# The gate matrices of four tokens, written one token behind the other

## The chip, the core and the metric
The kernel runs on one core of a Trainium2 chip. The core has a matrix engine (TensorE, PE in the profile; its weight loads are listed apart as PEld), a vector engine (VectorE, DVE), a scalar engine (ScalarE, ACT), GpSimd (POOL) and a sync engine (SyncE, SP) that issues most of the DMAs. Each works through its own list of instructions in order and waits on semaphores for the others. The metric is the device time of one execution in microseconds; a run's time is compared by its median.

## The reference
The program is one layer of a hybrid encoder block on 512 tokens of width 1024: an attention part with two branches, and behind it a product-key retrieval (PEER). The change touches the retrieval alone:

```
v1, i1 = lax.top_k(s1, 16); v2, i2 = lax.top_k(s2, 16)      # per token and head, 128 keys each
top, ci = lax.top_k(v1[..., :, None] + v2[..., None, :], 16) # best 16 of the pairs
eidx = e1 * 128 + e2; gate = softmax(top)                    # 8 heads x 16 experts of 16384
act = gelu(einsum('td,thkd->thk', x, expert_u[eidx]))
y = einsum('thk,thkd->td', gate * act, expert_v[eidx])
```

For every token 128 experts (8 heads of 16) are chosen out of 16384, and their rows of `expert_u` and `expert_v` are used with the weights gate times gelu.

## The kernel before
The 512 tokens form four groups of 128. Group 0 is done by gathers: for each of its 128 slots an indirect DMA on GpSimd's queue fetches one row per token (512 KB in all), VectorE takes the dot product with the token (`dot`, L1065) or adds the weighted row to a sum (`add`, L1077). The other three groups (384 tokens) are done densely: all 16384 experts are gone through in 128 blocks of 128. A block's `uT` rows are multiplied with the tokens (24 matmuls `pj`, L86 to L88, three fp32r products of high and low halves), gelu gives `am`, this is multiplied with the block's gates, and the product with `expert_v` is summed up in PSUM (`y`, L1231).

For the dense part the gates of a token are needed as a matrix of 128 x 128, first key by second key. The gate stage makes them, in the loop `for t0 in range(0, 128, T)` (from L1127), 32 steps of T = 4 tokens for each of three groups, 96 steps in all. The 128 slots of a token lie on the partitions. In a step VectorE writes
- two tiles `oh` (L1135): one-hot rows, 1 where the slot's first (second) key is e, an fp16 tile [128, 128, T] with the four tokens innermost;
- two tiles `og` (L1140): the first one-hot times the slot's gate, whose high and low fp16 halves are `gp[0]` and `gp[1]`.

TensorE then makes eight matmuls (L1147), two for each token, which sum over the slots; the weights are `oh[1][:, :, q + j]`, the moving columns `pcs[i][:, :, q + j]`, both with a step of four elements (8 bytes). ScalarE copies the four matrices of the step out of PSUM into the tile `stage` (L1149), with the token as the innermost index. After eight steps SyncE writes `stage` to HBM as `gd` (L1157), and the expert_v stage reads it back in pieces, `gch` (L1175).

What runs beside it: `oh` and `og` have three buffers each (OB = 3). The first 64 of the dense blocks' `uT` half are done ahead, from L1152 (`run_ahead`), most of them within the gate stage: SyncE loads `raw`, ScalarE rounds it to `whi` (L91), VectorE or GpSimd computes the rest `wlo` (L92), TensorE makes the 24 `pj`, ScalarE the gelu (L879), and the result goes to HBM as `gls`. In the last third of the stage `eidx` of group 0 is computed (L1125) and its first 16 gathers and dots are put out.

The order of instructions on each engine is not the order of the code. A scheduler sets it when the program is built, by costs of its own for every instruction; only GpSimd's order in the expert_v stage is fixed by hand. So the scheduler may answer the change of one instruction with another order of all of them.

Of the kernel before, what the change touches and what calls it, by code (L numbers as in the profile page):

```python
# [18 lines left out]
HF = mybir.dt.float16  # L19
# [3 lines left out]
OP = mybir.AluOpType  # L23
# [872 lines left out]
def peer(K, A, out):  # L896
    nc, cst, gen, Pool = K.nc, K.cst, K.gen, K.Pool
# [4 lines left out]
    RT, OB, SB, J0, GB = 8, 3, 2, 16, 4  # L902
# [12 lines left out]
    def ptr():  # L915
        return pe_.tile([128, 512], F32, name="pt", bufs=2)

    def pg():
        return pe_.tile([128, 512], F32, name="pg", bufs=2)
# [41 lines left out]
    def run_ahead():  # L961
        if K.ahead < NS:
            K.run_ahead(pmat(), pa.tile([128, ND], F32, name="am", bufs=4), nc.vector)
# [58 lines left out]
    def slots(p, a):  # L1022
        rb = ranks(p, a).rearrange("p h f k -> p (h f) k")

        eq = p.tile([128, 16, 16, 16], BF, name="eq", bufs=1)
        for r in range(16):
            nc.vector.scalar_tensor_tensor(eq[:, r], rb, float(r), ib[:, a, :, r, None].to_broadcast([128, 16, 16]),
                                           op0=OP.is_equal, op1=OP.mult)
        ev = eq.rearrange("p r s k -> p r (s k)")
        n = 8  # L1030
        while n > 1:
            nc.vector.tensor_tensor(ev[:, 0:n], ev[:, 0:n], ev[:, n:2 * n], op=OP.add)
            n //= 2
        ef = p.tile([128, 2, 128], F32, name="ef", bufs=2)
        nc.vector.tensor_tensor(ef.rearrange("p f (h k) -> p h f k", k=16), eq[:, 0].rearrange("p (h f) k -> p h f k", f=2),
                                eq[:, 1].rearrange("p (h f) k -> p h f k", f=2), op=OP.add)
        e = [ef[:, f, :] for f in range(2)]
        g = p.tile([128, 8, 16], F32, name="gate", bufs=2)
        nc.vector.tensor_tensor(g, top[:, a], top[:, a, :, 0:1].to_broadcast([128, 8, 16]), op=OP.subtract)
        nc.scalar.activation(g, g, AF.Exp)  # L1040
        z = small(8)
        nc.vector.tensor_reduce(out=z, in_=g, op=OP.add, axis=AX)
        rz = small(8)
        nc.vector.reciprocal(rz, z)
        nc.vector.tensor_tensor(g, g, rz[:, :, None].to_broadcast([128, 8, 16]), op=OP.mult)
        return e[0], e[1], g.rearrange("p h k -> p (h k)")
# [41 lines left out]
    def run_jobs(done):  # L1088
        while jobs and njobs - len(jobs) < done:
            jobs.pop(0)()  # L1090


    gt = K.wk = Pool("gates")
    T = 4
# [4 lines left out]
    def gathered_heads(hs):  # L1099
        for h in hs:  # L1100
            s0 = gt.tile([128, 4, 128], F32, name="sc0", bufs=2)
            nc.sync.dma_start(s0, A['sc0'][:, 2 * h:2 * h + 4, :])
            pair_top(gt, 0, h, lambda hh, half: s0[:, 2 * hh + half, :], 1)

    for b, a in enumerate(DT):
        if b:
            gathered_heads(range(4 * b - 4, 4 * b, 2))
        tr = []
        for n, t in enumerate(slots(gt, a)):
            p = ptr()  # L1110
            nc.tensor.transpose(p[:, :128], t, ident)
            s = gt.tile([128, 128], HF if n < 2 else F32, name=f"sT{n}", bufs=2)
            nc.scalar.activation(s, p[:, :128], AF.Copy, scale=1.0 if n < 2 else GS)
            tr.append(s)
        gT = tr[2]
        gp = []
        for i in range(2):
            q = gt.tile([128, 128], HF, name=f"gp{i}", bufs=2)
            nc.vector.tensor_copy(q, gT)
            if i == 0:  # L1120
                nc.vector.tensor_tensor(gT, gT, q, op=OP.subtract)
            gp.append(q)
        if b == 2:
            e1, e2, g = slots(gt, 0)
            nc.vector.scalar_tensor_tensor(eidx, e1, 128.0, e2, op0=OP.mult, op1=OP.add)  # L1125
            nc.vector.tensor_copy(gate0, g)
        for t0 in range(0, 128, T):  # L1127
            ts = slice(t0, t0 + T)
            tb = t0 % 32
            if tb == 0:  # L1130
                st = gt.tile([128, 128, 32], F32, name="stage", bufs=SB)
            oh = []
            for i in range(2):
                o = gt.tile([128, 128, T], HF, name=f"oh{i}", bufs=OB)
                nc.vector.tensor_tensor(o, tr[i][:, None, ts].to_broadcast([128, 128, T]), iota, op=OP.is_equal)  # L1135
                oh.append(o)
            pcs = []
            for i in range(2):
                o = gt.tile([128, 128, T], HF, name=f"og{i}", bufs=OB)
                nc.vector.tensor_tensor(  # L1140
                    o, oh[0], gp[i][:, None, ts].to_broadcast([128, 128, T]), op=OP.mult)
                pcs.append(o)
            for q in range(0, T, 4):
                p = pg()
                for j in range(4):
                    for i in range(2):
                        nc.tensor.matmul(p[:, j * 128:j * 128 + 128], oh[1][:, :, q + j], pcs[i][:, :, q + j],  # L1147
                                         start=i == 0, stop=i == 1)
                nc.scalar.activation(st[:, :, tb + q:tb + q + 4].rearrange("p e t -> p t e"),  # L1149
                                     p.rearrange("p (t e) -> p t e", t=4), AF.Copy, scale=1 / GS)  # L1150
            if t0 % 16 == RT:
                run_ahead()  # L1152
            if b == 2:
                run_jobs(J0 * (t0 + T) // 128)
            if tb == 28:
                for c in range(4):
                    nc.sync.dma_start(gd[c][4 * b + t0 // 32].rearrange("c p e t -> p c (e t)"),  # L1157
                                      st[:, 32 * c:32 * c + 32, :].rearrange("p (c e) t -> p c (e t)", e=8))
# [90 lines left out]
def block(tc, A, out):  # L1249
    with ExitStack() as ctx:  # L1250
        dram = ctx.enter_context(tc.tile_pool(name="dram", bufs=1, space=bass.MemoryType.DRAM))
        A['x1d'] = dram.tile([128, 4, 1024], F32, name="x1d")
        A['gd'] = [dram.tile([12, 4, 128, 8, 32], F32, name=f"gd{c}") for c in range(4)]
        A['gls'] = dram.tile([128, 128, 384], F32, name="gls")
        A['sc0'] = dram.tile([128, 16, 128], F32, name="sc0d")
        K = Ctx()
        setup(tc, ctx, K)
        front(K, A)
        peer(K, A, out)
# [29 lines left out]
```

## Time and profile before

| | |
|---|---|
| median of 3 runs | 2042.31 us (2037.0 to 2042.57) |
| profiled execution | 2043.98 us, its span 2042.2 us |
| busy in the span | TensorE 1918.3 us, VectorE 1585.0, ScalarE 844.9, GpSimd 821.9 |
| gate stage, from the first `oh` to the end of the last `og` | 874.9 to 1158.2 us |
| first `y` matmul | 1193.87 us |

Times in the rows are counted from the start of the span. A busy TensorE is not TensorE at its peak: matmuls are pipelined, so a matmul's own duration is longer than the step from one start to the next. A row that merges several instructions in succession gives the time from the first start to the last end.

### The profile page before, as it was taken

How to read it: one execution, taken by the hardware profiler on the slowest of the kernel's cores; microseconds unless marked ns; L12 is line 12 of the kernel's file. 1: busy time of each engine (PE TensorE's matmuls, PEld its weight loads, DVE VectorE, ACT ScalarE, POOL GpSimd, SP SyncE). 2: the span in 40 equal slices, each digit the busy share in tenths (PEclk: the TensorE clock that was granted, in tenths of full speed). 3: DMA queues.
4: the chain of work that ended last, by engine and by line, in shares of the span. 5: the costliest groups of instructions: out<-in, count | busy, mean ns of one | idle time of the engine just before them, and what ended most of it. 6: DMA issues, size and time to landing. Idle time of an engine off the chain costs nothing.

```text
span 2042.2 us, 28294 instructions
## 1 busy us (share of the span) xinstructions
PE 1918.3 (94%) x9858; PEld 1659.9 (81%) x9858; DVE 1585.0 (78%) x3212; ACT 844.9 (41%) x1330; POOL 821.9 (40%) x598
## 2 busy tenths in 40 slices
PE   6999999989899899999999998989898999999998
PEld 5987777777777788999999986968787878888886
DVE  8488585887766658998888778677877888878787
ACT  3444445646533333455666532333332333333232
POOL 2554332352244531000000545455555565746474
PEclk9999999999999899999999999999999999999999
DMA  7334142122246322646656998797979898989886
GB/s 261 90 115 123 52 145 57 37 84 87 63 150 213 140 88 88 190 151 214 225 194 209 336 340 310 272 338 257 357 280 323 288 331 299 338 291 327 320 318 256
DMA packets 199952, 436.80 MB, mean 214 GB/s; under 512 B 16465, under 2 KB 97666, under 8 KB 199682
## 3 DMA queue, kind: packets, MB, share of 16 engines
q1 hardware_dynamic: 162128, 298.65, 43.4%
q0 software_dynamic: 36864, 134.23, 18.0%
q10 hardware_dynamic: 818, 2.12, 0.3%
q8 instruction: 77, 1.26, 0.2%
q14 instruction: 65, 0.53, 0.1%
HBM read 391.95 MB, written 42.99 MB: 213 GB/s over the span
## 4 chain that ended last, share of the span: by engine, by line
PE 34%; DMA 19%; DVE 10%; issue 10%; POOL 5%; ACT 1%; SPq 0%; DVEq 0%; POOLq 0%; ACTq 0%
PE pj L86 6%; PE y L1231 6%; PE pj L87 6%; PE pj L88 6%; DMA gat<-expert_v,eidx 5%; PE pg L1147 5%; DMA raw<-uT 3%; DMA gat<-expert_u,eidx 3%; DMA am<-gls 3%; POOL gat L1059 3%; DVE wlo L92 2%; DMA raw<-expert_v 2%; POOL wlo L92 2%; PE pq L86 1%; PE pq L88 1%
## 5 line engine op out<-in xcount | busy, mean ns | idle before, releaser
L91 ACT ACTIVATE whi<-raw 128x1024 fp32r<-128x1024 f32 (+3 forms) x431 | 383.6, 894 | 610.4 <-DMA raw<-expert_v 242.6
L92 POOL TENSOR_TENSOR wlo<-raw,whi 128x1024 fp32r<-128x1024 f32 (+2 forms) x156 | 316.4, 2032 | 406.4 <-ACT whi L91 375.9
L92 DVE TENSOR_TENSOR wlo<-raw,whi 128x1024 fp32r<-128x1024 f32 (+3 forms) x275 | 333.7, 1217 | 136.5 <-ACT whi L91 136.1
L1059 POOL DMA_INDIRECT gat<-expert_u,eidx x128 | 162.6, 1270 | 464.6 <-DVE eidx L1125 343.5
L86 PE MATMUL pj<-h2h,whi 128*128 128x384 f32 x1008 | 344.4, 342 | 1.0 <-ACT am L879 1.0
L88 PE MATMUL pj<-h2h,wlo 128*128 128x384 f32 x1008 | 343.3, 341 | 0.0
L87 PE MATMUL pj<-h2l,whi 128*128 128x384 f32 x1008 | 343.3, 341 | 0.0
L1231 PE MATMUL y<-whi,al 128*128 128x512 f32 x768 | 239.3, 403 | 32.0 <-DVE al L92 32.0
L1231 PE MATMUL y<-wlo,ah 128*128 128x512 f32 x768 | 246.1, 401 | 9.2 <-POOL wlo L92 7.9
L1231 PE MATMUL y<-whi,ah 128*128 128x512 f32 x768 | 248.0, 400 | 5.5 <-ACT ah L91 5.4
L1059 POOL DMA_INDIRECT gat<-expert_v,eidx x128 | 172.8, 1350 | 132.8 <-DVE acc L1077 73.6
L1231 PEld LDWEIGHTS y<-whi,al 128*128 128x128 f32 x768 | 144.2, 190 | 76.7 <-DVE al L92 43.1
L1065 DVE SCALAR_TENSOR_TENSOR gscr<-gat,h2tok 128x1024 bf16<-128x1024 f32 x128 | 178.7, 1396 | 32.5 <-DMA gat<-expert_u,eidx 31.9
L86 PE MATMUL pj<-whi,hh 128*128 128x512 f32 (+2 forms) x512 | 193.0, 390 | 11.0 <-DVE gA L651 4.4
L1077 DVE SCALAR_TENSOR_TENSOR acc<-gat,wts,acc 128x1024 f32<-128x1024 f32 x127 | 173.9, 1369 | 31.6 <-DMA gat<-expert_v,eidx 31.1
L87 PE MATMUL pj<-wlo,hh 128*128 128x512 f32 (+2 forms) x512 | 196.0, 383 | 2.4 <-DVE wlo L92 2.3
L86 PEld LDWEIGHTS pj<-h2h,whi 128*128 128x128 f32 x1008 | 190.9, 189 | 4.2 <-ACT am L879 1.3
L87 PEld LDWEIGHTS pj<-h2l,whi 128*128 128x128 f32 x1008 | 190.7, 189 | 2.5
L88 PE MATMUL pj<-whi,hl 128*128 128x512 f32 (+2 forms) x512 | 192.0, 382 | 0.0
L88 PEld LDWEIGHTS pj<-h2h,wlo 128*128 128x128 f32 x1008 | 190.6, 189 | 0.4
L1231 PEld LDWEIGHTS y<-wlo,ah 128*128 128x128 f32 x768 | 146.6, 191 | 45.6 <-POOL wlo L92 8.3
L1231 PEld LDWEIGHTS y<-whi,ah 128*128 128x128 f32 x768 | 145.2, 191 | 36.8 <-ACT ah L91 7.3
(313 smaller groups left out, 3207.8 us busy)
## 6 DMA issues: line engine op xcount, KB each, us to landing
raw<-uT SPq DMA_DIRECT2D x128, 512.0 KB, 4.4
raw<-expert_v SPq DMA_DIRECT2D x128, 512.0 KB, 6.2
gd<-stage SPq DMA_DIRECT2D x48, 512.0 KB, 4.4
gch<-gd SPq DMA_DIRECT2D x16, 1536.0 KB, 11.2
raw<-w_in SPq DMA_DIRECT2D x88, 256.0 KB, 2.8
raw<-w_ada SPq DMA_DIRECT2D x64, 256.0 KB, 2.8
am<-gls SPq DMA_DIRECT2D x64, 192.0 KB, 6.2
gls<-am SPq DMA_DIRECT2D x62, 192.0 KB, 2.0
```

The source lines that it names most:

```text
L86: nc.tensor.matmul(ps, lh, rh, start=start, stop=False)
L87: nc.tensor.matmul(ps, lh, rl, start=False, stop=False)
L88: nc.tensor.matmul(ps, ll, rh, start=False, stop=stop)
L91: nc.scalar.activation(hi, raw, AF.Copy)
L92: (eng or nc.vector).tensor_tensor(lo, raw, hi.bitcast(F32), op=OP.subtract)
L1059: nc.gpsimd.indirect_dma_start(out=t, out_offset=None, in_=src, in_offset=bass.IndirectOffsetOnAxis(ap=eidx[:, s:s + 1], axis=0))
L1065: nc.vector.scalar_tensor_tensor(scr, t, 1.0, h2tok, op0=OP.mult, op1=OP.mult, accum_out=act[:, s:s + 1])
L1077: nc.vector.scalar_tensor_tensor(acc, t, wts[:, s:s + 1], acc, op0=OP.mult, op1=OP.add)
L1147: nc.tensor.matmul(p[:, j * 128:j * 128 + 128], oh[1][:, :, q + j], pcs[i][:, :, q + j], start=i == 0, stop=i == 1)
L1231: nc.tensor.matmul(ys[b][n], l[:, bs], r[:, n * 512:n * 512 + 512], start=n_ == 0 and i == 0, stop=n_ == 127 and i == 2)
```

## The change
The two tiles `og` are laid out as [128, T, 128], one token's 128 columns behind the other's. The multiply that writes them reads `oh[0]` through a view with its last two dimensions exchanged, and the gate with the token as the outer dimension, repeated over the 128 columns. The matmul's moving operand is `pcs[i][:, q + j, :]`. The one-hot tiles, the weights of the matmul and everything behind it stay as they are.

```diff
-                o = gt.tile([128, 128, T], HF, name=f"og{i}", bufs=OB)
+                o = gt.tile([128, T, 128], HF, name=f"og{i}", bufs=OB)
                 nc.vector.tensor_tensor(
-                    o, oh[0], gp[i][:, None, ts].to_broadcast([128, 128, T]), op=OP.mult)
+                    o, oh[0].rearrange("p e t -> p t e"), gp[i][:, ts, None].to_broadcast([128, T, 128]), op=OP.mult)
                 pcs.append(o)
             for q in range(0, T, 4):
                 p = pg()
                 for j in range(4):
                     for i in range(2):
-                        nc.tensor.matmul(p[:, j * 128:j * 128 + 128], oh[1][:, :, q + j], pcs[i][:, :, q + j],
+                        nc.tensor.matmul(p[:, j * 128:j * 128 + 128], oh[1][:, :, q + j], pcs[i][:, q + j, :],
                                          start=i == 0, stop=i == 1)
```

The scheduler also puts the instructions in another order, from the start of the gate stage on. On VectorE the end of the gate stage reads so before (`og_10923` to `og_10977` are the last two steps' tiles, `gscr,act` the dots of group 0; `eidx` stands 48 rows ahead of the last row here):

```order
L1140 TENSOR_TENSOR og_10923<-oh_10919,gp_10023 128x512
L1140 TENSOR_TENSOR og_10925<-oh_10919,gp_10026 128x512
L1065 SCALAR_TENSOR_TENSOR gscr,act<-gat,h2tok 128x1024
L1135 TENSOR_TENSOR oh_10973<-sT_10017,iota 128x512
L1140 TENSOR_TENSOR og_10975<-oh_10971,gp_10023 128x512
L1140 TENSOR_TENSOR og_10977<-oh_10971,gp_10026 128x512
L1065 SCALAR_TENSOR_TENSOR gscr,act<-gat,h2tok 128x1024
L92 TENSOR_TENSOR wlo<-raw,whi 128x1024
```

and now:

```order
L1140 TENSOR_TENSOR og_10923<-oh_10919,gp_10023 128x512
L1140 TENSOR_TENSOR og_10925<-oh_10919,gp_10026 128x512
L1140 TENSOR_TENSOR og_10975<-oh_10971,gp_10023 128x512
L1140 TENSOR_TENSOR og_10977<-oh_10971,gp_10026 128x512
L1032 TENSOR_TENSOR eq<-eq 128x512
L1035 TENSOR_TENSOR ef<-eq 128x8x2x16
L1125 SCALAR_TENSOR_TENSOR eidx<-ef 128x128
L1065 SCALAR_TENSOR_TENSOR gscr,act<-gat,h2tok 128x1024 x5
L1212 TENSOR_TENSOR am<-am,gch 128x384 x4
```

The five dots that stood between the last `og`, and `eidx` on which all gathers depend, have moved behind the last `og`.

On TensorE the last matmuls of the gate stage (the pair of tile `oh_10973`) are followed before by

```order
L1147 LDWEIGHTS oh_10973
L1147 MATMUL pg<-og_10977,oh_10973 128x128
L87 MATMUL pj<-h2l_6198,whi 128x384
L88 MATMUL pj<-h2h,wlo 128x384
L86 MATMUL pj<-h2h,whi 128x384
```

and now by

```order
L1147 LDWEIGHTS oh_10973
L1147 MATMUL pg<-og_10977,oh_10973 128x128
L1231 MATMUL y_12294<-whi,ah 128x512
L1231 MATMUL y_12295<-whi,ah 128x512
L1231 MATMUL y_12294<-wlo,ah 128x512
```

Before, 143 `pj` matmuls stand in this place, between the last gate matmul and the first `y`, and 1042 stand between the first gate matmul and the last. Now there are 1183 between them and none behind; the last ten gate steps (80 matmuls) stand together.

## Rows read from the trace of the kernel before

**Rows 1.** The page: busy us (share) and instructions; the gathers' group, mean ns of one.
```profile
PE 1918.3 (94%) x9858; PEld 1659.9 (81%) x9858; DVE 1585.0 (78%) x3212; ACT 844.9 (41%) x1330; POOL 821.9 (40%) x598
...
L1059 POOL DMA_INDIRECT gat<-expert_u,eidx x128 | 162.6, 1270 | 464.6 <-DVE eidx L1125 343.5
```
**Rows 2.** Busy time by stretch: PE, PEld, DVE, ACT, POOL, clock, DMA share, GB/s.
```profile
874.90:1158.20 283.30, 283.30 (x1861) 264.30 (x1860) 242.72 (x676) 172.01 (x199) 16.51 (x11) 1.00 0.63 215
1158.20:1165.00 6.80, 6.80 (x48) 6.51 (x46) 5.83 (x9) 4.47 (x7) 3.85 (x4) 1.00 0.98 340
1165.00:1194.00 29.00, 24.76 (x144) 24.44 (x142) 13.20 (x17) 8.57 (x13) 13.41 (x10) 0.99 1.03 376
1194.00:2042.00 848.00, 798.49 (x3696) 680.44 (x3696) 677.90 (x752) 272.90 (x377) 477.94 (x301) 0.99 0.86 307
```
**Rows 3.** Lines 1147 and 1140: count, ns min/median/max, first and last start.
```profile
L1147 PE MATMUL pg<-og,oh x768: 278/297/304, 889.8 to 1164.5; 128*128 128x128 f16 x192
...
L1140 DVE TENSOR_TENSOR og<-oh,gp x192: 402/418/2598, 885.9 to 1157.7; 128x512 f16<-128x512 f16 x192
```
**Rows 4.** Waits from 885 to 1170: us in total, times, longest.
```profile
DVE og L1140 <- PE pg L1147: 21.4, 28, 2.5
...
DVE wlo L92 <- ACT whi L91: 19.1, 20, 5.5
```
**Rows 5.** Order of time on TensorE, three places: start us, us, count at the end.
```profile
207.04 1.00 PE L568 MATMUL pt<-va,eT 128*128 128x64 f32 x8
...
717.36 1.05 PE L991 MATMUL pt<-skt,f 128*128 128x128 f32 x8
...
961.26 1.11 PE L1147 MATMUL pg<-og,oh 128*128 128x128 f16 x8
```
**Rows 6.** Groups by line and shape: count, busy us, mean ns, idle before.
```profile
L1032 DVE TENSOR_TENSOR eq<-eq 128x512 bf16<-128x512 bf16 x4 | 1.7, 416 | 0.0
...
L1196 DVE TENSOR_TENSOR yo<-acc,g 128x512 f32<-128x512 f32 x2 | 1.3, 677 | 0.0
...
L1149 ACT ACTIVATE stage<-pg 128x512 f32<-128x512 f32 x96 | 107.6, 1134 | 76.6 <-PE pg L1147 74.3 <-issue 2.1
...
L988 ACT ACTIVATE f<-pq 128x512 f32<-128x512 f32 x16 | 9.6, 598 | 30.2 <-PE pq L88 30.2
...
L92 DVE TENSOR_TENSOR wlo<-raw,whi 128x1024 fp32r<-128x1024 f32 x45 | 54.7, 1220 | 13.7 <-ACT whi L91 13.7
...
L1027 DVE SCALAR_TENSOR_TENSOR eq<-rb,ib 128x256 bf16<-128x256 bf16 x48 | 16.8, 415 | 0.0
```
**Rows 7.** Order of time on VectorE, end of the gate stage.
```profile
1129.88 0.28 DVE L1125 SCALAR_TENSOR_TENSOR eidx<-ef 128x128 uint32<-128x128 f32 x1
...
1157.39 0.75 DVE L1140 TENSOR_TENSOR og<-oh,gp 128x512 f16<-128x512 f16 x2
...
1170.98 1.22 DVE L1065 SCALAR_TENSOR_TENSOR gscr<-gat,h2tok 128x1024 bf16<-128x1024 f32 x1
1172.12 0.08 DVE L1065 DVE_READ_ACCUMULATOR gscr<-gat,h2tok 128x1 f32 x1
...
1183.92 3.40 DVE L1065 SCALAR_TENSOR_TENSOR gscr<-gat,h2tok 128x1024 bf16<-128x1024 f32 x1 [1.33 <-DMA gat<-expert_u,eidx]
...
1199.16 0.75 DVE L1075 TENSOR_SCALAR acc<-gat,wts 128x1024 f32<-128x1024 f32 x1
```
**Rows 8.** The chain that ended last: start us, us, what.
```profile
1163.89 0.95 PE pg L1147 x8
...
1175.63 16.89 DMA gch<-gd
...
1193.87 9.98 PE y L1231 x36
```
**Rows 9.** DMA issues: queue, kind, count, KB, median us to landing.
```profile
gch<-gd SPq DMA_DIRECT2D x16, 1536.0 KB, 11.2
...
gat<-expert_u,eidx POOLq DMA_INDIRECT x128, 7.1
```

## The prediction
> **What bounds the kernel now.** I read the page's busy shares first: TensorE 94% of the span, VectorE 78% [rows 1]. The change touches one stage, the gate stage (lines 1127 to 1158), so I then cut the span at its borders. From the first `oh` at 874.9 to the end of the last `og` at 1158.2 us it lasts 283.3 us [rows 2]. TensorE is never idle in it, at the full granted clock; VectorE works 242.72 us and is idle for 40.6. The waits of the stage say for whom: VectorE waits 21.4 us for gate matmuls before an `og`, which has three buffers, and 19.1 us for ScalarE's `whi` before a `wlo` [rows 4]. The stage is TensorE's, with a margin of 40.6 us on VectorE.
>
> **What a gate matmul pays.** There are 768, from 889.8 us on [rows 3]. Eight in a row take 1.11 us, the last alone 0.297, so one follows the other after (1.11 - 0.297) / 7 = 0.116 us. Each is a weight load of 128 columns and a pass of 128 moving columns; which of the two sets 0.116 the profile doesn't say. The fp32 score matmuls of line 991, both operands contiguous, go at (1.05 - 0.275) / 7 = 0.111; the 64-column matmuls of line 568, half the moving columns behind the same weight load, at (1.00 - 0.275) / 7 = 0.104 [rows 5]. A 384-column `pj` matmul takes 24.76 / 144 = 0.172 [rows 2], so 128 contiguous columns alone would need 0.057. Halving the moving columns hardly shortens the step: the weight load sets the pace, and the change leaves the weight, `oh[1][:, :, q + j]`, at its step of four elements. I take a gain of nothing; the bounds are 0 and 768 x (0.116 - 0.057) = 45 us (fp32 rows stand in for fp16 ones, so the upper end is open). A loss has no source: contiguous columns replace strided ones.
>
> [...]
>
> **What `og` pays.** The 192 multiplies (L1140) write 512 fp16 elements in 0.418 us [rows 3], as an add of 512 bf16 elements with unit steps does (0.416); a multiply of 512 fp32 elements takes 0.677 [rows 6]. In the change `oh[0]` is read at a step of four and the gate at a step of zero. No row shows such a multiply. Lower bound: 0.418, if the fast rate survives. Upper bound: ScalarE's eviction in this stage, which writes with a step of 128 bytes, takes 1.134 against 0.598 for a contiguous 512 [rows 6], 0.536 more; on 0.677 that makes 1.213. I take 0.677, the nearest row in engine and operation: 192 x (0.677 - 0.418) = 49.7 us of VectorE's time, bounds 0 and 152.6.
>
> [...]
>
> **What the order does.** The rows of the order show a second change. Before, 1042 `pj` matmuls stand between the first and the last gate matmul, and 143 behind the last, before the first `y`. Now 1183 stand between, none behind, and the last ten of the 96 gate steps stand together with no `pj` among them. On VectorE five dots (L1065, 1.30 each [rows 7]), `eidx` and two halvings (1.1) go behind the last `og`, and three `wlo` (1.22 [rows 6]) come in front: 242.7 - 6.5 - 1.1 + 3.7 + 49.7 = 288.5 us of work up to the last `og`, with at most the 19 us of `whi` waits (I leave 12), so 300.5, to 1175.4 if nothing else held it.
>
> TensorE is later than that. Before, its work in the stretch is 1042 x 0.172 + 768 x 0.116 = 268 of the 275 us to the last gate matmul's end, 1163.89 + 0.95 = 1164.8 [rows 8], nearly all of it. 141 more `pj` are 141 x 0.172 = 24.3 us, so the last gate matmul can't end before 1189.1, and the ten steps (0.94 each) can't begin before 1179.7. TensorE stays the bound up to there. Then it turns: VectorE has three steps ready, as its buffers allow, and must make seven: 14 `og` of 0.677, 14 `oh` of 0.418, 16 products of the selection at 16.8 / 48 = 0.35 and two halvings of 1.9 in all, 22.8; instructions in a row overlap by about 0.085 (two `og` take 0.75) [rows 6, 7], which takes off 2.4. So the last `og` ends at about 1200 and the last gate matmul at 1201, 36 us late.
>
> Behind it two chains lead on:
> - To the first `y`. Before it came 29.0 us behind the last gate matmul (1193.87): eviction, the `gd` writes, a `gch` load of 16.89 [rows 8], whose median is 11.2 [rows 9]. The 143 `pj` covered these 29 us; now nothing does and TensorE stands still. With fewer loads beside it I give `gch` half of the difference back: 26, so `y` starts at 1227, 33 us late (bounds 30 and 36).
> - To the first weighted sum. `eidx` stood at 1129.88 [rows 7] and the 16 gathers and dots behind it lay under the stage. Now it comes at 1201. A gather lands after 7.1 [rows 9] behind an issue of 1.3 [rows 1], so the first dot is at 1209.5. A dot takes 1.22 + 0.08 = 1.30; where dots ran freely, from 1170.98 to 1183.92, five steps took 12.94, 2.6 each [rows 7]. Sixteen need 21 to 41 us; with 31 they end at 1240, and the sum starts at 1242 instead of 1199.16, 42 late (bounds 32 and 53).
>
> GpSimd issues the 16 gathers behind its last `wlo` and has nothing else then; on SP `gd` and `gch` keep their order, with the `uT` loads ahead. What follows, 848 us [rows 2], has the same instructions and is shifted. With TensorE at 798.5 of the 848 the `y` chain weighs more than the sums: I take 36, between 33 and 42. The profiled execution took 2043.98 us, so 2080.0 by its time; the median of the runs is 1.7 lower: 2078.3.
>
> **The rivals.**
> The moving side was the limit, `og` at 0.677. TensorE's floor falls by up to 45 us to 1144, VectorE's 1175.4 (1163.4 without waits) decides, and the last gate matmul ends between 1165 and 1177. `y` is then 0 to 12 us late and the first sum -4 to 28 (from 1164.5 or 1176.5 on, as above): 2044 to 2066, in the middle 2056. It decides once a gate step is under about 0.098, where 768 x 0.018 = 14 us bring TensorE under VectorE. For it speaks that both bounds come from fp32 rows; against it the 64-column row.
>
> A dearer `og`: the strided read costs more than a cycle per element. It decides from about 0.75 us, where VectorE passes TensorE's 1189. At 1.213 VectorE needs 391.4 us and with 5 of waits ends at 1271, 113 late; two gate steps follow instead of 6.7 us of mixed work, so 2042 + 108 = 2150; at half the surcharge 2102. For it speaks the eviction; against it that this step is 128 bytes and a write, the new one 8 bytes and a read.
> [...]
>
> Faster, the other sign: `og` keeps 0.418 and the moving side was the limit. VectorE needs 238.8 us and 12 of waits, to 1126; TensorE's floor of 1144 decides, 21 us early, and `eidx` stays where VectorE can hide the dots: 2021. It takes an `og` under about 0.5 and a step under 0.08; the lost unit steps and the 64-column row both speak against it.
>
> **How the numbers follow.** Order and `og` as above: 0.48, its own range 2064 to 2095. Moving side: 0.23. Dearer: 0.16, 2095 to 2150. Faster: 0.06. A rest of 0.07 where several waits shrink at once and nothing is seen. No change is what a measurement can't tell, 0.3% or 6.1 us: faster than 2036 has 0.06; within, 0.12 (the rest and the low fifth of the moving case); slower 0.82. The range leaves out the fast case and the upper part of the dear one: 2041 to 2112.
>
> **What would show it.** Right: gate matmuls still 0.11 to 0.12 apart; `og` 0.67 to 0.70 in 192 rows; ten gate steps in a row at the end with TensorE waiting for `og`; the last near 1201; then over 20 us of idle TensorE before the first `y`; `eidx` and the dots in one block. Wrong: a gate step under 0.1, an `og` at 0.42 or over 0.75, a last gate step before 1180, or a loss that lies behind the first `y`.

## The result: 1.5% slower, and the profile after

The changed kernel takes 2072.4 us (2066.1 to 2075.3, median of 4) against 2042.2 us of the kernel before beside it: ratio 1.0151, 95% interval 1.0134 to 1.0169. The forecast was 2078.3. The number is near, but the way to it was another: the page after answers to [rows 1], and TensorE has less work, not the same.

```profile
span 2069.2 us, 28278 instructions
...
PE 1888.3 (91%) x9858; PEld 1621.5 (78%) x9858; DVE 1631.5 (79%) x3212; ACT 843.7 (41%) x1330; POOL 823.4 (40%) x598
```

TensorE's busy time falls by 30.0 us, from 1918.3, and the span still grows by 27.0, so its idle time grows by 57. VectorE gains 46.5 us of work. The two instructions that the change touches, with count, ns min/median/max and first and last start (before in [rows 3]):

```profile
L1147 PE MATMUL pg<-og,oh x768: 216/220/315, 887.1 to 1171.8; 128*128 128x128 f16 x192
...
L1140 DVE TENSOR_TENSOR og<-oh,gp x192: 669/690/2689, 882.3 to 1170.4; 128x512 f16<-128x512 f16 x192
```

`og` went from 418 to 690 ns, as forecast. But the gate matmul shortened too, and in order of time on TensorE eight in a row take 0.61 us where [rows 5] had 1.11, and the last pieces of the stage 0.91 for seven, at a granted clock of 0.50 (last section):

```profile
961.13 0.61 PE L1147 MATMUL pg<-og,oh 128*128 128x128 f16 x8 [0.96 <-ACT stage L1149]
...
1171.22 0.91 PE L1147 MATMUL pg<-og,oh 128*128 128x128 f16 x7 [0.19 <-DVE og L1140]
1200.09 1.22 PE L1231 MATMUL y<-whi,ah 128*128 128x512 f32 x2 [27.97 <-ACT ah L91]
...
1208.38 0.34 PE L87 MATMUL pj<-h2l,whi 128*128 128x384 f32 x1
1224.85 1.22 PE L1231 MATMUL y<-wlo,ah 128*128 128x512 f32 x2 [16.13 <-POOL wlo L92]
```

The step is (0.61 - 0.22) / 7 = 0.056 us instead of 0.116. The last three rows show two holes in TensorE's work: 28 us before the first `y`, which comes only 6.2 us later than before [rows 8], and 16 us between 1208 and 1225, before a second expert's `y`. The waits from 871 to 1260 us (total, times, longest) tell the same, and that the stage has changed hands: VectorE's 21.4 us for gate matmuls [rows 4] have become 3.1, and TensorE waits for `og`.

```profile
PE y L1231 <- ACT ah L91: 28.0, 1, 28.0
PE y L1231 <- POOL wlo L92: 16.8, 2, 16.1
PE pg L1147 <- DVE og L1140: 13.3, 14, 5.4
...
DVE og L1140 <- PE pg L1147: 3.1, 5, 1.5
```

Busy time by stretch (columns as in [rows 2]) for the kernel before, and then for the changed one:

```profile
874.90:1172.00 297.10, 297.10 (x1947) 277.82 (x1946) 250.71 (x686) 178.97 (x207) 24.39 (x16) 1.00 0.65 221
1172.00:1200.00 28.00, 23.76 (x123) 22.23 (x122) 15.77 (x26) 8.38 (x14) 10.31 (x8) 0.94 0.98 357
1200.00:1225.00 25.00, 25.00 (x121) 21.76 (x119) 23.20 (x20) 8.62 (x12) 16.44 (x11) 1.00 0.93 325
```

```profile
874.90:1172.00 297.10, 281.66 (x2029) 253.56 (x2027) 286.07 (x655) 179.40 (x211) 9.94 (x3) 0.97 0.59 199
1172.00:1200.00 28.00, 0.13 (x2) 0.00 (x0) 7.58 (x14) 1.53 (x4) 8.64 (x9) 0.50 0.95 334
1200.00:1225.00 25.00, 8.78 (x27) 6.76 (x27) 18.83 (x31) 2.16 (x6) 14.19 (x11) 0.64 0.65 212
```

Idle time of TensorE: 15.4 + 27.9 + 16.2 = 59.5 us in these three stretches, against 4.2 before. That is where the 57 us lie; after 1225 TensorE is idle for 49.7 us in the one and 50.7 in the other. VectorE works 286 of the 297 us up to 1172: it is the bound of the stage now. The chain that ended last (start us, us, what) shows what it hands on, and in order of time on GpSimd why the second hole ends when it does:

```profile
1168.76 2.41 DVE og L1140 x4
...
1172.00 0.30 DVE eidx L1125
...
1172.58 6.62 DMA gat<-expert_u,eidx
...
1204.31 1.06 POOL gat L1059
...
1222.88 1.95 DVE wts L1070
```

```profile
1189.31 0.94 POOL L1059 DMA_INDIRECT gat<-expert_u,eidx  x1 [1.06 <-DVE gscr L1065]
1204.31 1.80 POOL L1059 DMA_INDIRECT gat<-expert_u,eidx  x1 [14.06 <-DVE gscr L1065]
...
1220.27 1.82 POOL L1059 DMA_INDIRECT gat<-expert_v,eidx  x1 [1.10 <-DVE gscr L1065]
1222.11 2.68 POOL L92 TENSOR_TENSOR wlo<-raw,whi 128x1024 fp32r<-128x1024 f32 x1
```

`eidx` comes at 1172.0 instead of 1129.9 [rows 7], behind the last `og`. A gather has four buffers, so GpSimd must wait for VectorE's dots; those stand on VectorE behind the `am` multiply, which waits for `gch` until 1198.9:

```profile
1198.88 1.96 DVE L1212 TENSOR_TENSOR am<-am,gch 128x384 f32<-128x384 f32 x4 [9.84 <-DMA gch<-gd]
```

GpSimd's queue then holds the split `wlo` of an expert behind 16 + 2 gathers, and TensorE needs that `wlo`.

### The profile page after: what moved, and what is told of

Read it like the earlier page. It is cut to its first block, busy times and chain, and to the rows that moved or that the text cites. A ratio compares the mean times of both kernels' runs of the same rounds, so it can differ in the third digit from the quotient of the medians.

```text
span 2069.2 us, 28278 instructions
## 1 busy us (share of the span) xinstructions
PE 1888.3 (91%) x9858; PEld 1621.5 (78%) x9858; DVE 1631.5 (79%) x3212; ACT 843.7 (41%) x1330; POOL 823.4 (40%) x598
## 4 chain that ended last, share of the span: by engine, by line
PE 32%; DMA 18%; DVE 13%; issue 10%; POOL 5%; ACT 1%; SPq 0%; DVEq 0%; POOLq 0%; ACTq 0%
PE y L1231 7%; PE pj L86 6%; PE pj L87 6%; PE pj L88 6%; DMA gat<-expert_v,eidx 5%; DMA am<-gls 3%; DMA gat<-expert_u,eidx 3%; POOL gat L1059 3%; DMA raw<-uT 3%; DMA raw<-expert_v 2%; DVE og L1140 2%; DVE wlo L92 2%; POOL wlo L92 2%; PE pq L86 1%; PE pq L88 1%
## 5 line engine op out<-in xcount | busy, mean ns | idle before, releaser
L92 DVE TENSOR_TENSOR wlo<-raw,whi 128x1024 fp32r<-128x1024 f32 (+3 forms) x275 | 320.9, 1170 | 114.8 <-ACT whi L91 114.5
L1059 POOL DMA_INDIRECT gat<-expert_u,eidx x128 | 161.2, 1260 | 190.6 <-DVE gscr L1065 65.2
```

What stands on the lines that cost most here:

```text
L92: (eng or nc.vector).tensor_tensor(lo, raw, hi.bitcast(F32), op=OP.subtract)
L1059: nc.gpsimd.indirect_dma_start(out=t, out_offset=None, in_=src, in_offset=bass.IndirectOffsetOnAxis(ap=eidx[:, s:s + 1], axis=0))
```

## The experiments

Two theories stood at the start. **A**: the moving side of the gate matmul was the limit and is faster now; VectorE, with the dearer `og`, bounds the stage, and what hangs on the late `eidx` makes the loss. **B**, the forecast's own: the strided weight load sets the pace, and the shorter step comes from something else. Ratios below are to runs of the kernel before on the same chip, with 95% intervals. The first three kernels take the change apart, with one caution: wherever the scheduler lays out the instructions anew, a kernel changes in its order too.

**x2, contiguous columns alone**, on the kernel before.

```diff
-  oh[1][:, :, q + j], pcs[i][:, :, q + j],
+  oh[1][:, :, q + j], pcs[i].rearrange("p e t -> p (e t)")[:, (q+j)*128:(q+j)*128+128],
```

> The kernel before with its og tiles written as before, but the matmul's moving operand is 128 neighbouring elements of the tile instead of every fourth one (the four tokens' gate values are mixed, so the gate matrices are not the reference's). The instruction order of the kernel before is kept. Theory A (the moving side set the pace of the gate matmuls): the step of a run of eight falls from 0.116 us to about 0.056, the 768 gate matmuls give back about 46 us, VectorE's 40 us of waits in the stage go and the stage ends 30 to 38 us sooner: 2004 to 2020 us. Theory B (the strided weight load sets the pace, as the prediction had it; the step fell in the changed kernel for another reason): step 0.116 and 2042 us, within 6.

Measured 2009.0 us, ratio 0.9862 (0.9835 to 0.9889). Eight gate matmuls, on TensorE in order of time:

```profile
959.54 0.64 PE L1147 MATMUL pg<-og,oh 128*128 128x128 f16 x8
```

The step is (0.64 - 0.22) / 7 = 0.060, with `og` still at 421 ns and the weights still strided. `eidx` keeps its place some 30 us ahead of the last `og` (1098.6, 1128.2), so the order is that of the kernel before. Theory A, and the change's own idea is worth 1.4%.

**x9, contiguous weights alone**, the counterpart.

```diff
-  oh[1][:, :, q + j], pcs[i][:, :, q + j],
+  oh[1].rearrange("p e t -> p (e t)")[:, (q+j)*128:(q+j)*128+128], pcs[i][:, :, q + j],
```

> The kernel before, but the weights of the gate matmuls are 128 neighbouring elements of the one-hot tile instead of every fourth one (the tokens' rows are mixed, so the gate matrices are not the reference's); the moving columns stay strided. Theory A (the moving side alone sets the pace): step 0.116 and 2036 to 2048 us. Theory B (the strided weight load sets or shares the pace): step well below 0.116 and 2000 to 2030 us.

One run: 2042.4 us, beside 2042.1. The step is (1.09 - 0.294) / 7 = 0.114:

```profile
960.00 1.09 PE L1147 MATMUL pg<-og,oh 128*128 128x128 f16 x8
```

Theory B falls.

**x1, the dear `og` with the strided columns.** On the kernel before, with 32-bit gates.

```diff
+                w = gt.tile([128, 128], F32, name="gw", bufs=1)
+                nc.vector.tensor_copy(w, q)
...
-            gp.append(q)
+                gp.append(w)          # second piece: gT itself, F32
```

> The kernel before with its layout and its strided moving columns, but the gate values that og multiplies with are 32 bits wide, which should bring og from 0.41 us to 0.67 to 0.7 as in the changed kernel. Theory A (in the changed kernel VectorE bounds the stage, and the faster matmul buys nothing): gate matmuls at 0.116 us, TensorE's and VectorE's work about equal at 285 to 300 us, 2070 to 2085 us, so at most 10 us above the changed kernel's 2072. Rival (the faster matmul did pay in the changed kernel): two engines without slack hold each other up, stage over 320 us, 2095 us or more.

Measured 2093.8 us, ratio 1.0266 (1.0237 to 1.0295): between the two expectations, nearer to the rival. `og` takes 686 ns, and unlike in the changed kernel VectorE still waits for TensorE (871 to 1250 us):

```profile
DVE oh L1139 <- PE pg L1151: 19.4, 26, 1.9
...
DVE og L1144 <- PE pg L1151: 11.2, 11, 2.1
```

The scheduler puts `eidx` behind the last `og` here too (1202.0 us, where the kernel before has it at 1129.9), so x1 has the dear `og` and the late `eidx` together, and its 2.7% are the price of both. With that the parts nearly add: -1.4% for the columns, +2.7% for `og` with its order, +1.5% for all. My theory that the faster matmul buys nothing once VectorE bounds the stage was wrong: without it the two engines hold each other up, the stage lasts 328 us instead of 300, and it is worth 1.0266 - 1.0151 = 1.15%, some 23 us.

The next four ask what behind the stage makes the loss.

**x4, the first GpSimd splits given to VectorE.**

```diff
-  split(vh, vl, raw, nc.gpsimd if e % 4 == 1 else nc.vector)
+  split(vh, vl, raw, nc.gpsimd if e % 4 == 1 and n_ > 8 else nc.vector)
```

> The changed kernel, with the GpSimd splits of the last stage's first eight experts given to VectorE. Theory A (in the changed kernel the second expert's matmuls lose 16 us to a GpSimd split that stands behind 16 gathers): that wait goes, 2054 to 2062 us. Rival (the split is only the last of several that end together; VectorE has the split behind the same gathers): another wait takes its place, 2068 to 2074 us.

Measured 2063.0 us, ratio 1.0127 (1.0100 to 1.0153), an interval that overlaps the changed kernel's. The wait for GpSimd is gone and another stands in its place:

```profile
PE y L1231 <- DVE wlo L92: 13.3, 1, 13.3
```

The time lies between the two expectations. The queue was not all of the wait; by the two ratios the gain is some 5 us and isn't settled.

**x5, projections kept back as a cover** for the 28 us hole. `issue_after` ties only the order on TensorE.

```diff
+            if b == 2 and t0 == 84:
+                hm = mm               # a gate matmul of this step
...
-    while K.ahead < NS:
+    while K.ahead < NS - 6:
         run_ahead()
+    with K.tc.issue_after(hm.ins):
+        while K.ahead < NS:
+            run_ahead()
```

> The changed kernel, with the last six projection blocks that are made ahead tied behind a gate matmul of the last token groups, so that 144 projection matmuls (144 x 0.173 = 25 us) stand between the last gate matmul and the first weighted sum, as they do in the kernel before; the order on VectorE and GpSimd stays that of the changed kernel. Theory A (the stage's end leaves TensorE 28 us without work, and the lost cover is most of the loss): the 28 us wait shrinks to 3 to 8 us, later work is 25 us smaller, 2046 to 2054 us. Rival (the loss is VectorE's longer stage; TensorE only moves its idle time, and the gathers behind the stage set what follows): 2064 to 2074 us.

Measured 2074.5 us, ratio 1.0160 (1.0134 to 1.0185): no gain. Waits from 871 to 1260 us:

```profile
PE y L1236 <- POOL wlo L92: 21.9, 2, 19.7
PE pg L1147 <- DVE og L1140: 19.5, 42, 1.4
...
PE y L1236 <- ACT ah L91: 0.3, 1, 0.3
```

The hole of 28 us was filled (0.3 left), and TensorE waits 5 us longer for the split and 6 longer for `og`; `eidx` stays at 1171.4, the first weighted sum comes at 1229.5. So the cover of the idle time before the first `y` was not what was lost; whether the chain behind `eidx` was, the next run asks.

**x10, `eidx` early.**

```diff
-  nc.vector.scalar_tensor_tensor(eidx, ...)
+  ei = nc.vector.scalar_tensor_tensor(eidx, ...)
+  with K.tc.issue_after(ei.ins) if b == 2 and t0 >= 80 else nullcontext():
       oh = [] ...   # one-hot and og tiles of the step
```

> The changed kernel, with the last twelve token groups' one-hot and og instructions tied behind the instruction that makes the gather indices, so that VectorE makes them 54 rows ahead of its last og, as in the kernel before (46), and does six dot products inside the stage. Theory A (the loss is that the indices now come last on the engine that bounds the stage, and the gather chain with its GpSimd queue starts 42 us late): first weighted accumulation at 1200 to 1212 instead of 1225, GpSimd split no longer waited for, 2048 to 2060 us. Rival (VectorE has no slack, so what is moved ahead delays the last gate matrices by as much, and with them everything behind): 2066 to 2076 us.

Measured 2051.9 us (median of 10), ratio 1.0043 (1.0025 to 1.0061): two thirds of the loss are back. On VectorE:

```profile
1155.06 0.29 DVE L1125 SCALAR_TENSOR_TENSOR eidx<-ef 128x128 uint32<-128x128 f32 x1
...
1183.82 2.49 DVE L1141 TENSOR_TENSOR og<-oh,gp 128x512 f16<-128x512 f16 x4
...
1217.70 0.75 DVE L1075 TENSOR_SCALAR acc<-gat,wts 128x1024 f32<-128x1024 f32 x1
```

No `y` waits for GpSimd any more. The first sum was expected by 1212 and stands at 1217.7, and the last `og` is 15 us later; the profiled execution is the slowest of the ten (2061.9), so its rows show less than the median gains. Even so it tells the two chains apart: the first `y` comes 12 us later than in the changed kernel (1212.3), the first sum 7 us sooner, and the time falls.

**x11, x10 with the edits of x4 and x5 added.**

> The changed kernel with three orders repaired at once: gather indices early on VectorE, six projection blocks held behind the last token groups, and the first GpSimd splits of the last stage on VectorE. Theory A (the price beyond VectorE's longer stage is all in these orders): what is left is a stage of 300 us against 283 with the idle ends covered, 2036 to 2050 us, within 10 us of the kernel before. Rival (the repairs take each other's gain, as each covers the same wait): 2055 to 2066 us.

Measured 2055.0 us, ratio 1.0065 (1.0042 to 1.0087): the intervals of x10 and x11 overlap, so the repairs don't add. TensorE waits 32.8 us for `og` instead. Some 9 to 13 us stay in both orders; that they are the price of VectorE's longer stage is likely, but no run shows it apart.

The profiled executions of these kernels say which chain carries the loss. Against the one of the kernel before, in us:

| | first `y` later by | first sum later by | span longer by |
|---|---|---|---|
| changed | 6.2 | 25.7 | 27.0 |
| x1 | 37.4 | 56.3 | 54.4 |
| x5 | 8.1 | 30.3 | 27.6 |
| x10 | 18.5 | 18.5 | 18.0 |
| x11 | 10.5 | 11.9 | 9.2 |
| x4 | 5.2 | 23.4 | 13.5 |

In the first five rows the span goes with the first sum to within 3 us, and not with the first `y`. x4 is 10 us shorter than its sum says; its profiled execution (2058.1) is near the fastest of its six, which may be part of it. x12 below falls short as well (`y` 19.9 sooner, sum 9.6 later, span 3.7 longer). So the chain behind `eidx` carries most of the loss, not every microsecond.

The last five look for a layout with both: contiguous columns and a cheap `og`.

**x3, the sides exchanged.** Only one tile of a step, the first one-hot tile, is written token by token.

```diff
-  oh[1][:, :, q + j], pcs[i][:, :, q + j],
+  pcs[i][:, :, q + j], oh[0][:, q + j, :],
...
-  o, oh[0], gp[i][:, None, ts]...          # og, old layout
+  o, oh[1], gp[i][:, None, ts]...
...
+  o = gt.tile([128, T, 128], HF, name="oh0", bufs=OB)
+  nc.vector.tensor_tensor(o, tr[0][:, ts, None]..., iotr[:, None, :]..., op=OP.is_equal)
```

> The sides of the matmul are exchanged: og is built from the other one-hot tile in the old layout (all rows of stride 1) and loaded as weights, and the first one-hot tile is written token by token and is the contiguous moving side. Only the one oh tile has a broadcast of stride 0 along its innermost axis. Theory A (moving side set the pace; a stride of 0 in the innermost axis costs VectorE the fast rate): gate matmul step 0.056, oh0 0.67 to 0.70 us and oh1 and og 0.38 to 0.42, VectorE's stage 243 + 96 x 0.28 = 270 us against 283 before, no long waits for TensorE: 2020 to 2035 us, faster than both. If a stride of 0 alone does not cost the fast rate: oh0 at 0.4, stage about 245 us, 2000 to 2015. Theory B (the strided weight load sets the pace): step 0.116, TensorE as before and 2042 to 2060.

Measured 2033.7 us, ratio 0.9972 (0.9952 to 0.9992), as expected. The tile with the step of zero costs the fast rate, its neighbours keep it:

```profile
L1138 DVE TENSOR_TENSOR oh<-sT,iotr x96: 677/687/769, 871.8 to 1157.5; 128x512 f16<-128x512 f16 x96
...
L1142 DVE TENSOR_TENSOR oh<-sT,iota x96: 377/421/505, 873.6 to 1154.7; 128x512 f16<-128x512 f16 x96
```

**x6, x3 with three projection blocks kept back** (as x5, behind step 112).

> The kernel with the sides exchanged, and its last three projection blocks tied behind a gate matmul of the last token groups (169 projection matmuls stand behind the stage). Theory A (its 28 us of idle TensorE behind the stage can be filled): 2034 - 20 to 25 = 2009 to 2014 us, faster than both kernels. Rival (VectorE and the gathers behind the stage become the bound): 2025 to 2034 us.

Measured 2028.3 us, ratio 0.9930 (0.9906 to 0.9955): against x3's interval hardly settled, and far from theory A's 2009 to 2014. TensorE waits 25.4 us for `og` and 11.5 for GpSimd's split. As in x5, the hole moves.

**x7, x3 with the token-outer tile made by four instructions**, for which the keys `tr[0]` are kept in 32 bits.

```diff
+  for j in range(T):
+      nc.vector.tensor_scalar(o[:, j, :], iotr, tr[0][:, t0+j:t0+j+1], None, op0=OP.is_equal)
```

> The kernel with the sides exchanged, and the token-outer one-hot tile made by four instructions of 128 columns that compare the index row with one value for each partition, instead of one of 512 columns with a broadcast of stride 0. If four small ones go at the fast rate and overlap, 0.13 us or less each: 0.52 against 0.60 us a tile, VectorE 8 us shorter, 2022 to 2034 us. If their fixed time rules, 0.2 us or more each: 19 us longer on VectorE, 2040 to 2055 us.

One run: 2035.6 us. Four cost 74.7 / 96 = 0.78 us of VectorE a tile, one of x3 66.8 / 96 = 0.70; I had expected at least 2040 from that, so the sum was too steep. No gain.

**x12, which operand costs `og` its rate.** On the changed kernel.

```diff
-  o, oh[0].rearrange("p e t -> p t e"), gp[i][:, ts, None]...
+  o, oh[0].rearrange("p e t -> p t e"), iota...   # 128 x 512 neighbouring elements
```

> The changed kernel, but og multiplies the one-hot tile, still read 8 bytes apart, by 128 x 512 neighbouring elements of the index tile instead of the gate values broadcast with stride 0 (so the gates are left out of the gate matrices). It separates the two operands that the change gave og an innermost step other than 1. If the read 8 bytes apart costs the fast rate by itself: og 0.67 to 0.70 us and 2064 to 2078 us. If only the broadcast of stride 0 costs it: og 0.40 to 0.45, and 2005 to 2035 us.

```profile
L1140 DVE TENSOR_TENSOR og<-oh,iota x192: 637/689/2899, 871.0 to 1154.0; 128x512 f16<-128x512 f16 x192
```

The read 8 bytes apart alone costs the rate (0.689 us by median), as x3's step of zero alone does (0.687). The one time, 2047.7 us, lies below the expected range; `og` no longer needs the gates, and its stage starts 11 us earlier (871.0 against 882.3), so the time says nothing about `og`.

**x8, pairs of tokens.** Two tokens side by side, so that VectorE's rows end in two neighbouring elements and the moving columns are 4 bytes apart.

```diff
+  def pair(x):
+      return x[:, ts].rearrange("p (a b) -> p a b", b=2)[:, :, None, :].to_broadcast([128, 2, 128, 2])
...
+  # io2 = iota[:, None, :, 0:2].to_broadcast([128, 2, 128, 2])
+  o = gt.tile([128, 2, 128, 2], HF, name="oh0", bufs=OB)
+  nc.vector.tensor_tensor(o, pair(tr[0]), io2, op=OP.is_equal)
...
+  o = gt.tile([128, 2, 128, 2], HF, name=f"og{i}", bufs=OB)
+  nc.vector.tensor_tensor(o, oh[0], pair(gp[i]), op=OP.mult)
...
-  oh[1][:, :, q + j], pcs[i][:, :, q + j],
+  oh[1][:, :, q + j], pcs[i][:, (q + j) // 2, :, (q + j) % 2],
```

> The kernel before, with the first one-hot tile and the two og tiles laid out in pairs of tokens: the two tokens of a pair lie next to each other, so that every row that VectorE works along still ends in two neighbouring elements, and a matmul's moving columns are 4 bytes apart instead of 8. The result is the reference's and the order is that of the kernel before. If VectorE keeps its fast rate (og 0.40 to 0.45 us) and 4 bytes apart is as good as contiguous for the moving side: gate matmul step 0.056 and 2003 to 2016 us, as the kernel with the contiguous view, faster than both. If the moving side pays for 4 bytes as for 8: step 0.116, 2036 to 2048. If VectorE loses its rate with rows of two: og 0.67 or more, three slow tiles, 2075 us or more.

Measured 2010.2 us (2004.7 to 2013.3), ratio 0.9834 (0.9815 to 0.9854): faster than both kernels, and the same gain as x2 with the reference's result. Busy us and mean ns by group, and eight gate matmuls:

```profile
L1147 DVE TENSOR_TENSOR og<-oh,gp 128x512 f16<-128x512 f16 x192 | 80.6, 436 | 4.4 <-PE pg L1153 3.9
L1142 DVE TENSOR_TENSOR oh<-sT,iota 128x512 f16<-128x512 f16 x96 | 43.1, 451 | 0.1
L1139 DVE TENSOR_TENSOR oh<-sT,iota 128x512 f16<-128x512 f16 x96 | 39.5, 420 | 0.0
```

```profile
958.04 0.66 PE L1153 MATMUL pg<-og,oh 128*128 128x128 f16 x8
```

VectorE pays nothing (436 ns a mean `og`, 430 before), and the step is (0.66 - 0.22) / 7 = 0.063.

## Why the prediction was right in the sum and wrong in its steps

**What `og` pays: right.** 0.677 us was taken from one fp32 row and 0.690 measured; 49.7 us of VectorE's time forecast, 128.6 - 79.8 = 48.8 found by the groups of both traces. That the fast rate goes with the unit steps was my estimate, and no row of the kernel before shows it; x3 (0.687 us), x12 (0.689) and, for one 32-bit input, x1 (0.686 and 0.687) do, against 0.418 before. The dear rival, which needed an `og` from 0.75 us on, falls with the measured 0.690; what "a cycle per element", by which it was put, comes to on VectorE no run shows.

**"The weight load sets the pace": wrong**, and the step of the sum that failed. It rested on line 568, where half the moving columns hardly shortened the step; those are fp32 rows, and I had marked the bound as open at its upper end, then taken the lower. The trace before already showed that their weight loads are others, 0.192 us by median against 0.117:

```profile
L568 PEld LDWEIGHTS pt<-va,eT x192: 186/192/338, 156.5 to 324.8; 128*128 128x128 f32 x192
...
L1147 PEld LDWEIGHTS <-oh x768: 111/117/138, 889.8 to 1164.4; 128*128 128x128 f16 x192
```

x2 (a step of 0.060 us with contiguous columns) and x9 (0.114 with contiguous weights) show that the moving read made 0.116; what bounds line 568 no run shows. The pitch of 8 bytes does cost the moving read: 0.114 to 0.116 us a step at 8 bytes, 0.063 at 4 (x8).

**TensorE's floor of 1189 and the last gate matmul at 1201: wrong with it.** They came at 1171.8, where VectorE put them: the 300.5 us worked out for VectorE's stage "if nothing else held it" were 1171.1 - 871.2 = 299.9.

**The idle TensorE before the first `y`:** over 20 us were named as a sign, and 28 came. But `y` was 6 us late, not 33, and in x5 the hole was filled and nothing was gained (1.0160 against 1.0151).

**The first weighted sum:** 42 us late forecast, 25.7 found, with `eidx` and the dots in one block behind the stage as the order said. This is the chain that carried most of the loss (x10 and the table), and the forecast gave it less weight than `y`. It overlooked why the two are one: "GpSimd issues the 16 gathers behind its last `wlo` and has nothing else then". It has the splits of the last stage in its queue, and `y` needs them.

**So the sum came out by luck: two errors met.** A gain of up to 45 us was put at nothing, so the stage's end was put 30 us too late, and `y` and the first sum with it. Against that stood the price of being late, 36 between `y`'s 33 and the sum's 42, a third of the way. With the late ends that came, the same weighting would give 6.2 + (25.7 - 6.2) / 3 = 12.7 us, about 2055 (an estimate); the profiled execution lost 27. Three of the signs named for being wrong came: a step under 0.1, a last gate step before 1180, and a loss that lies mostly behind the first `y`.

The rival with a fast moving side had the right mechanism: the last gate matmul between 1165 and 1177, `y` 0 to 12 late and the sum -4 to 28 late; all three came within. It ended at 2044 to 2066 and missed 2072 since its price, 2 to 24 us, also lay between the two late ends, where the loss followed the later one.

## What to carry to other kernels

A strided operand should be priced on each engine that touches it: here 4 bytes of pitch satisfy TensorE's moving read (0.063 us a step, against 0.056 to 0.060 contiguous) and a run of two neighbouring 16-bit elements satisfies VectorE (0.436 us a mean `og`, against 0.430), so a layout in pairs gives both what a full transpose takes from one of them. Where a change makes another engine the bound, look at what that engine does last in the stage: a short instruction with a long chain behind it (`eidx`) weighed more here than the busy time added; moving it forward gave back two thirds of the loss. Follow an in-order queue to the end of the chain before saying that it has nothing else to do.

## What the runs showed of the hardware

- Moving columns of 128 x 128 fp16 matmuls: 0.114 to 0.116 us a step at a pitch of 8 bytes, 0.063 at 4, 0.056 to 0.060 contiguous; with the weights at a pitch of 8 bytes the step was 0.116 (before), with contiguous weights 0.114 (x9).
- VectorE, 512 fp16 elements, two inputs: 0.418 to 0.421 us by median where all innermost steps are one (before, x2, x3), 0.436 by mean in runs of two (x8, against 0.430 before); 0.687 by median with a step of zero in one input (x3), 0.689 with one of 8 bytes (x12), 0.686 and 0.687 with one 32-bit input (x1).
- TensorE's granted clock falls to 0.50 at the end of the changed kernel's stage, where the engine, mostly waiting for `og`, was idle for 13.5 of the 22 us from 1150 on; before, it was 1.00 up to 1172 us. The two stretches in which it falls (columns as in [rows 2]):

```profile
1150.00:1160.00 10.00, 2.80 (x24) 1.85 (x24) 10.00 (x28) 3.91 (x4) 0.00 (x0) 0.71 0.59 211
1160.00:1172.00 12.00, 5.70 (x40) 3.98 (x40) 11.93 (x26) 4.25 (x4) 0.00 (x0) 0.50 0.00 0
```

So the engine that had become the waiting one was here also slower at its own work: the last seven gate matmuls took 0.91 us, where eight took 0.61 at a clock of 1.00. That its idle time lowers the clock no run shows apart.
